# A hybrid encoder layer on one core: reordered gate and attention steps, two early weights in other tiles, normalisations at high priority

## The chip, the cores and the metric

The kernel runs on one core of one Trainium2 chip, in one launch. The metric is the device time of one execution in microseconds (us), median over the runs. The engines are TensorE (PE in the rows), VectorE (DVE), ScalarE (ACT) and GpSimd (POOL); SyncE (SP) issues most of the DMAs.

## The reference

One layer of an encoder over a sequence of 1024 tokens with 1024 features, all float32:

```python
u = rmsnorm(h, norm_mix_pre)
proj = u @ w_in                       # q, k, v, gate ga, low-rank za of the GLA heads; q, k, v of the window heads
o_a = gla_chunked(fwd) + flip(gla_chunked(bwd))          # 4 heads, chunks of 64, both directions
o_a = rms_per_head(o_a) * gla_norm * silu(ga)
o_s = banded_window_gqa(qs, ks, vs, sink, rel_table)     # 8 query heads, 2 kv heads, |i-j| <= 128
h = h + rmsnorm(concat([o_a, o_s]) @ w_out, norm_mix_post)
z = rmsnorm(h, norm_mlp_pre) @ w_up                      # 1024 x 4096
ff = square(relu(z)) @ w_down                            # 4096 x 1024
out = h + rmsnorm(ff, norm_mlp_post)
```

## The kernel before, in words

Every large matrix product is made of three: each float32 operand is split into a rounded high part (a cast) and the rest (a subtraction), and hi·hi, hi·lo and lo·hi are summed in PSUM. A weight that comes in therefore costs a DMA into a raw tile, a cast of 128x1024 on ACT (line 93) and a subtraction on DVE (line 196). PSUM is four tags of two banks each: "mm", "ga", "tr", "lg".

A scheduler sets the order of each engine's instructions when the program is built: of what could go next it takes what stands first in the program, and what is written under `tc.high_priority()` ahead of that. On the chip each engine runs its list in order. The program's order in the middle of the kernel is a string, `ORDER`, of tokens:

- `g<h><half>` is the gate projection of head h for one half of the tokens: 24 matmuls of 512 columns (line 222, `pin`), Silu on ACT (L648), a product on DVE (L649), and a store. Its weights are the tiles `wh` and `wl` (two buffers each), and the next head's weights are fetched when both halves of a head are done. `g0<half>` to `g3<half>` are eight such blocks.
- `S` is one step of the window attention, a unit of 128 queries and one kv head (16 units, software-pipelined): four logit products (`pl`, L545 and L546, tag "lg"), each reduced on DVE (L548) and put through the exponential on ACT (L551), a normalisation (L562), four groups of three transposes (`ppt`, L171, tag "tr"), each cast on ACT (L93) and subtracted on DVE (L571), and the product with v (`pvo`, L579 to L583, tag "lg"), copied out by ACT (L585). Silu and the exponential need different ACT tables, and a switch is an `ACT_TABLE_LOAD`.
- `W<k>`, `w<k>` load and split the k-th block of rows of w_out (512 KB; blocks 4 to 7 in two DMAs of 256 KB). Their raw tiles, of two buffers, are those of the gate weights.
- `M<n>` is w_out's product for tokens 128n to 128n+127, 48 matmuls of 512 columns (`pm`, L809 and L814), behind a load of the mixer's output (L800), a cast of it on ACT (L801) and a subtraction (L802). `N<n>` is the normalisation behind it (two squares on ACT at L825, a power on POOL at L180 and L181, DVE at L831 and L833, another square, DVE at L840), and `T<n>` transposes the result for the MLP (`pzt`, eight transposes, with copies on ACT at L856 and L859 and DVE work at L862 to L868).

After the string the MLP's first products stand in the program. `early(j)` brings columns of w_up into a raw tile and splits them into parts of `r1` and `r2`; `t_split` splits sums of the transposed tokens (L881, L882); `product(p, j)` is 12 matmuls of 512 columns (L995, into `pa`, `pb`, `pc`), written (p,j) below. The eighth normalisation takes two of the splits between its parts:

```python
early(0)
early(1)
t_setup()
wout_norm(7, pms[7], (lambda: t_split(0), lambda: t_split(1)))
```

In the profile the stretch of the gates is 285 to 347 us, that of M0 to M6 about 347 to 442 us, and the tail, from M7 to the first products of the MLP, 442 to 482 us. What follows to the end, some 600 us, is the MLP, whose program the change leaves as it is but for the place of one weight.

Of the kernel before, what the change touches and what calls it, by code (L numbers as in the profile page):

```python
# [20 lines left out]
S = 1024  # L21
# [50 lines left out]

ORDER = (
# [4 lines left out]
)  # L78


def hybrid_layer(tc, x, g_mix_pre, w_in, w_gu_f, b_g_f, w_gu_b, b_g_b, gla_norm, sink, rel_bias, w_out,
# [16 lines left out]
    with ExitStack() as ctx:  # L98
# [93 lines left out]
        def split(raw, hi, lo):  # L192
            k = spl_i[0]
            spl_i[0] += 1
            C(W_HI[k] if k < len(W_HI) else "a", hi, raw)
            E(W_LO[k] if k < len(W_LO) else "v").tensor_sub(lo, raw, hi)
# [231 lines left out]
        for tok in START.split():  # L428
            k, a = tok[0], tok[1:]
# [4 lines left out]
            elif k in "zvk":  # L434
                q0, n = int(a[0]), int(a[1])
# [14 lines left out]
        W2 = e2(8.25, 1056)  # L450
# [322 lines left out]
        wb = {}  # L773
# [40 lines left out]
                    nc.tensor.matmul(pm[c], lhsT=OTL[:, kt, :], rhs=woh[kt][:, sl], start=False, stop=kt == 7)  # L814
            return pm

        def wout_norm(n, pm, between=(None, None)):
            GB1, GB2 = wb["GB1"], wb["GB2"]

            TB, XB = wb["OT"] if n == 7 else (wb["TB"], wb["XB"])  # L820
            Q("xres").dma_start(XB, x[0, n * 128:(n + 1) * 128, :])
            s2 = tiny(2)
            for c in range(2):
                junk = wb["AR"](16, 512) if n > 4 else TB[:, c * 512:c * 512 + 512]
                nc.scalar.activation(junk, pm[c], AF.Square, scale=1.0 / 32, accum_out=s2[:, c:c + 1])  # L825
            r = rstd_of(s2[:, 0:1], 1, s2[:, 1:2])
            if between[0]:
                between[0]()
            for c in range(2):
                sl = slice(c * 512, c * 512 + 512)  # L830
                nc.vector.scalar_tensor_tensor(out=TB[:, sl], in0=pm[c], scalar=r, in1=GB1[:, sl],  # L831
                                               op0=ALU.mult, op1=ALU.mult)
            nc.vector.tensor_add(XB, XB, TB)  # L833
            Q("hds").dma_start(hd[n], XB)
            ss = tiny(1)
            nc.scalar.activation(TB, XB, AF.Square, scale=1.0 / 32, accum_out=ss)
            r = rstd_of(ss)
            if between[1]:
                between[1]()
            nc.vector.scalar_tensor_tensor(out=TB, in0=XB, scalar=r, in1=GB2, op0=ALU.mult, op1=ALU.mult)  # L840

        def wout_tr(n):
# [41 lines left out]
        pms = {}  # L884
        for tok in order:
            k, a = tok[0], tok[1:]
            if k == "K":
                proj_qk(int(a), "K", KD, 1.0)
            elif k == "Q":
                proj_qk(int(a), "Q", QD, 0.125)  # L890
            elif k == "H":
                gates(int(a))
            elif k in "VER":
                {"V": gla_v, "E": gla_e, "R": gla_r}[k](int(a))
            elif k in "CBF":
                {"C": gla_c, "B": gla_o, "F": gla_f}[k](int(a[0]), int(a[1]))
            elif k == "s":
                proj_qs(int(a))
            elif k == "S":
                swa_step()  # L900
            elif k == "L":
                load_bias()
            elif k in "Ww":
                fetch_wo(int(a))
            elif k == "g":
                ga_half(int(a[0]), int(a[1]))
            elif k == "M":
                pms[int(a)] = wout_mm(int(a))
            elif k == "N":
                wout_norm(int(a), pms[int(a)])  # L910
            elif k == "T":
                wout_tr(int(a))
            else:
                raise Stop(tok)
# [9 lines left out]
        def double(k):  # L924
            r, o = (r1, r2)[k % 4 // 2], 8 * (k % 2)
            return r(o, 1024), r(o + 4, 1024)
# [12 lines left out]
        def load_up(dst, f):  # L939
            nc.sync.dma_start(dst.rearrange("p (a b) -> p a b", a=8), w_up_r[:, :, f * 128:(f + 1) * 128])  # L940
# [2 lines left out]
            return t[:, i * 512:i * 512 + 512].rearrange("p (a b) -> p a b", a=4)  # L943

        def early(j):
            load_up(wb["RW"], j)
            split(double(j), wb["RW"])

        early(0)
        early(1)  # L950
        t_setup()
        wout_norm(7, pms[7], (lambda: t_split(0), lambda: t_split(1)))

        PA = [bank("mm", "pa0"), bank("mm", "pa1"), bank("ga", "pa2"), bank("ga", "pa3")]
        PB = [bank("lg", "pb0"), bank("lg", "pb1")]
# [20 lines left out]
        where = {}  # L976
# [9 lines left out]
            return PA[j % 4] if p in (1, 6, 7, 4) else PB[j % 2] if p == 2 else PC[j % 2]  # L986

        def product(p, j):
            (hi, lo), i = where[p, j] if p != 4 else (single(j), 0)
            hi, lo = k4(hi, i), k4(lo, i)  # L990
            bh, bl = U[tokens[p]]
            ps_ = bank_of(p, j)
            for n, (a, b) in enumerate(((hi, bh), (hi, bl), (lo, bh))):
                for kt in range(4):
                    nc.tensor.matmul(ps_, lhsT=a[:, kt, :], rhs=b[:, kt, :], start=p in (1, 2, 5) and n == 0 and kt == 0,  # L995
                                     stop=n == 2 and kt == 3, skip_group_check=True)
# [230 lines left out]
        for n, (i, u) in enumerate(steps):  # L1227
            p, _, _, banks = plan[i]
# [93 lines left out]
```

## Time and profile before

| what | value |
|---|---|
| median of 3 runs | 1080.88 us (1080.38 to 1081.57) |
| profiled execution, device time | 1081.89 us |
| its span in the trace | 1080.2 us |
| mean granted TensorE clock | 0.997 |
| PE busy | 1046.8 us (97%) |
| DVE busy | 723.5 us (67%) |
| ACT busy | 545.0 us (50%) |
| POOL busy | 154.7 us (14%) |
| chain that ended last | PE 82%, DVE 7%, ACT 3%, DMA 3% |

Busy shares are averages over the whole span. A matmul's busy time overlaps the next one's, so the distance from one start to the next tells what it takes on PE; where that is longer than the usual distance for its shape, PE lost the difference. The device time is 1.7 us longer than the span, for what lies around it.

### The profile page before, as it was taken

Reading aid. Unit: us, or ns where it says so; the run is one execution under the profiler, and the core shown is the slowest. Engines: PE = TensorE matmul, PEld = TensorE weight load, DVE = VectorE, ACT = ScalarE, POOL = GpSimd, SP = SyncE. Lnnn points to the kernel's source line nnn. Section 1 sums busy time; section 2 is a strip of 40 time slices with the busy share of each in tenths; the row PEclk is TensorE's granted clock in tenths of the full one; section 3 lists DMA queues with packets and bytes.
Section 4 is the critical chain, followed back from the end, with each engine's and each line's share of the span. In section 5 each row is a group of like instructions: output and inputs, shape, how many; then the busy total and the mean of one; then the engine's idle time right before and its main releaser. Section 6 shows DMA issues by size and latency. Waiting matters only on the chain.

```text
span 1080.2 us, 13661 instructions
## 1 busy us (share of the span) xinstructions
PE 1046.8 (97%) x4950; PEld 853.4 (79%) x4950; DVE 723.5 (67%) x1101; ACT 545.0 (50%) x952; POOL 154.7 (14%) x246
## 2 busy tenths in 40 slices
PE   6999999999998999989999999999999999999997
PEld 4787787887886887778888888888778888888885
DVE  8659457788778567799656656663479764547565
ACT  5565324633877456566555555554434334345342
POOL 4211012111211111102211212121100000002001
PEclk9999999999999999999999999999999999999999
DMA  7355443613667433547553635447983332345622
GB/s 229 114 158 164 133 124 83 147 40 82 178 182 182 120 121 103 160 121 237 195 171 118 193 117 172 151 138 241 381 320 99 97 98 98 117 137 185 204 98 98
DMA packets 138421, 164.82 MB, mean 153 GB/s; under 512 B 17089, under 2 KB 93889, under 8 KB 138354
## 3 DMA queue, kind: packets, MB, share of 16 engines
q1 hardware_dynamic: 109394, 110.46, 32.9%
q0 software_dynamic: 22560, 37.76, 11.9%
q10 hardware_dynamic: 6400, 15.73, 4.5%
q8 instruction: 39, 0.64, 0.3%
q14 instruction: 28, 0.23, 0.1%
HBM read 111.47 MB, written 52.45 MB: 152 GB/s over the span
## 4 chain that ended last, share of the span: by engine, by line
PE 82%; DVE 7%; ACT 3%; DMA 3%; issue 3%; POOL 1%; SPq 0%; ACTq 0%; DVEq 0%; POOLq 0%
PE pa L995 15%; PE pa L1219 15%; PE pin L222 11%; PE pc L995 8%; PE pb L1219 6%; PE pc L1219 6%; PE pm L809 3%; PE pb L995 3%; PE pm L814 2%; PE pkv L222 2%; PE ppt L171 2%; DMA wd<-in_w_down_dram 1%; PE pl L545 1%; PE pl L546 1%; PE pvo L579 1%
## 5 line engine op out<-in xcount | busy, mean ns | idle before, releaser
L1219 PE MATMUL pa<-r 128*128 128x512 f32 x768 | 175.1, 389 | 0.8 <-DVE r L1164 0.8
L1219 PEld LDWEIGHTS pa<-r 128*128 128x128 f32 x768 | 144.0, 188 | 31.4 <-DVE r L1164 1.6
L1161 ACT CAST r<-ra 128x1024 fp32r<-128x1024 f32 x56 | 58.9, 1052 | 166.0 <-PE pa L1219 94.2
L1163 DVE TENSOR_TENSOR r<-ra,r 128x1024 fp32r<-128x1024 f32 x56 | 68.4, 1222 | 106.7 <-ACT r L1161 106.7
L995 PE MATMUL pa<-th,r 128*128 128x512 f32 x384 | 102.3, 389 | 1.3 <-ACT sn L1010 1.3
L995 PEld LDWEIGHTS pa<-th,r 128*128 128x128 f32 x384 | 72.0, 188 | 16.6 <-ACT sn L1010 1.7
L222 PE MATMUL pin<-uth,wh 128*128 128x512 f32 x256 | 69.7, 398 | 0.0
L1219 PE MATMUL pb<-r 128*128 128x512 f32 x288 | 69.7, 390 | 0.0
L1219 PE MATMUL pc<-r 128*128 128x512 f32 x288 | 69.2, 389 | 0.0
L222 PE MATMUL pin<-utl,wh 128*128 128x512 f32 x256 | 68.2, 394 | 0.0
L222 PE MATMUL pin<-uth,wl 128*128 128x512 f32 x256 | 68.0, 394 | 0.0
L1164 DVE TENSOR_TENSOR r<-wd,r 128x1024 fp32r<-128x1024 f32 x52 | 63.3, 1217 | 4.4 <-ACT r L1162 4.4
L809 PE MATMUL pm<-wo,b 128*128 128x512 f32 x256 | 65.0, 396 | 0.0
L1219 PEld LDWEIGHTS pb<-r 128*128 128x128 f32 x288 | 53.9, 188 | 11.8 <-DVE r L1164 0.7
L1219 PEld LDWEIGHTS pc<-r 128*128 128x128 f32 x288 | 54.0, 188 | 11.2
L1069 DVE TENSOR_TENSOR r<-su,r 128x1024 fp32r<-128x1024 f32 x32 | 39.0, 1220 | 28.8 <-ACT r L1068 28.8
L180 POOL TENSOR_SCALAR cst<-cst 128x1 f32<-128x1 f32 x16 | 9.9, 618 | 337.5 <-ACT wd L1186 292.8
L1162 ACT CAST r<-wd 128x1024 fp32r<-128x1024 f32 x52 | 54.6, 1050 | 6.0 <-DMA wd<-in_w_down_dram 6.0
L1003 ACT ACTIVATE ar<-ar 128x512 f32<-128x512 f32 x42 | 26.5, 632 | 58.3 <-DVE ar L1014 58.3
L222 PEld LDWEIGHTS pin<-uth,wl 128*128 128x128 f32 x256 | 47.7, 188 | 9.0
L222 PEld LDWEIGHTS pin<-utl,wh 128*128 128x128 f32 x256 | 47.7, 188 | 8.9
L809 PEld LDWEIGHTS pm<-wo,b 128*128 128x128 f32 x256 | 47.1, 188 | 8.6
(291 smaller groups left out, 2121.5 us busy)
## 6 DMA issues: line engine op xcount, KB each, us to landing
ra<-hss SPq DMA_DIRECT2D x32, 512.0 KB, 3.7
wd<-in_w_down_dram SPq DMA_DIRECT2D x28, 512.0 KB, 9.1
hss<-ar POOLq DMA_DIRECT2D x54, 256.0 KB, 4.8
ra<-hsx SPq DMA_DIRECT2D x24, 512.0 KB, 3.6
hsx<-ar POOLq DMA_DIRECT2D x47, 256.0 KB, 2.8
ra<-in_w_up_dram SPq DMA_DIRECT2D x16, 512.0 KB, 4.1
rb<-in_w_up_dram SPq DMA_DIRECT2D x16, 512.0 KB, 5.7
raw<-in_w_in_dram SPq DMA_DIRECT2D x14, 512.0 KB, 4.5
```

Source lines behind the costliest of these rows:

```text
L171: nc.tensor.transpose(dst_bank[:, i * 128:(i + 1) * 128], s, ident)
L222: nc.tensor.matmul(p[:, cs], lhsT=a[:, kt, :], rhs=b[:, kt, cs], start=k == 0, stop=k == 23)
L809: nc.tensor.matmul(pm[c], lhsT=OTH[:, kt, :], rhs=w_[kt][:, sl], start=(w_ is woh and kt == 0), stop=False)
L814: nc.tensor.matmul(pm[c], lhsT=OTL[:, kt, :], rhs=woh[kt][:, sl], start=False, stop=kt == 7)
L995: nc.tensor.matmul(ps_, lhsT=a[:, kt, :], rhs=b[:, kt, :], start=p in (1, 2, 5) and n == 0 and kt == 0, stop=n == 2 and kt == 3, skip_grou ...
L1003: nc.scalar.activation(x_, x_ if src is None else src, AF.Relu)
L1069: late.append(lambda: nc.vector.tensor_sub(d[1], src, d[0]))
L1161: nc.scalar.copy(sd[0], ra[n % 2])
L1162: nc.scalar.copy(td[0], src)
L1163: nc.vector.tensor_sub(sd[1], ra[n % 2], sd[0])
L1164: nc.vector.tensor_sub(td[1], src, td[0])
L1219: nc.tensor.matmul(banks[t], lhsT=sd[a][:, c * 512 + t * 128:c * 512 + t * 128 + 128], rhs=td[b][:, c * 512:c * 512 + 512], start=p in (1, ...
```

## The change

Three edits. In `ORDER`, the steps between `g01` and `M0` are rearranged: the halves 0 of the gates (`g10`, `g30`, `g20`) come earlier, each with `W` tokens behind it, and of the six `S` there three remain; the three others now stand one behind `T1` and two behind `T2`. `early(3)` uses the tile `TB`, which the normalisations free, as its raw tile in place of `RW`, and `early(2)` is split in two halves, of which product (1,2)'s part goes to `single(0)`, a part of `r1` that nothing else holds so early. And `wout_norm` runs under `tc.high_priority()`, with the two splits behind the eighth and not between its parts.

```diff
-        "Q1 F11 E2 V2 C20 C21 R2 S S B20 B21 E3 V3 F21 F20 C30 C31 R3 S S g00 B30 B31 F31 g01 S F30 S W0 S "
-        "g11 g30 W1 g31 g10 W2 W3 g20 w4 w5 S S w6 g21 S w7 M0 N0 M1 T0 S N1 M2 T1 N2 M3 T2 N3 M4 T3 S S M5 "
-        "N4 T4 M6 N5 T5 N6 M7 T6 "
+        "Q1 F11 E2 V2 C20 C21 R2 S S B20 B21 E3 V3 F21 F20 C30 C31 R3 S S g00 B30 B31 F31 g01 F30 S W0 g10 W1 "
+        "g30 S W2 g11 W3 g20 w4 w5 g31 S w6 w7 g21 M0 N0 M1 T0 S N1 M2 T1 S N2 M3 T2 S S N3 M4 T3 S S M5 N4 T4 M6 "
+        "N5 T5 N6 M7 T6 "
...
-        def wout_norm(n, pm, between=(None, None)):
+        def wout_norm(n, pm):
...
-            if between[0]:
-                between[0]()
...
-            if between[1]:
-                between[1]()
...
-                wout_norm(int(a), pms[int(a)])
+                with tc.high_priority():
+                    wout_norm(int(a), pms[int(a)])
...
         def early(j):
-            load_up(wb["RW"], j)
-            split(double(j), wb["RW"])
+
+            raw = wb["TB" if j == 3 else "RW"]
+            load_up(raw, j)
+            if j == 2:
+                hi, lo = double(j)
+                split(single(0), raw[:, 0:512])
+                split((hi[:, 512:1024], lo[:, 512:1024]), raw[:, 512:1024])
+            else:
+                split(double(j), raw)
...
-        wout_norm(7, pms[7], (lambda: t_split(0), lambda: t_split(1)))
+        with tc.high_priority():
+            wout_norm(7, pms[7])
+        t_split(0)
+        t_split(1)
...
-            (hi, lo), i = where[p, j] if p != 4 else (single(j), 0)
+            (hi, lo), i = where[p, j] if p != 4 and (p, j) != (1, 2) else (single(j if p == 4 else 0), 0)
```

What this does to the engines' lists, at three places. (A number behind a name is the buffer's; the same tile may have another in the two kernels.)

**Place 1, ACT where head 2's gate weights are cast.** Of the kernel before, ACT's list: `pin_2685` is g31, `pin_2720` is g10, `wh_2715` are head 2's weights, `wo` is w_out.

```order
L93 CAST wo_2554<-raw_2748 128x1024
L551 ACTIVATE s2_85,cst_63<-s2_85,cst_63 128x384
L557 ACTIVATE cst_63<-cst_63 128x4
L585 COPY s3_525<-pvo_2604 64x512
L648 ACT_TABLE_LOAD
L648 ACTIVATE g3_517<-pin_2685 128x512
L93 CAST wh_2715<-raw_2713 128x1024
L93 CAST wo_2554<-raw_2752 128x1024
L648 ACTIVATE g3_517<-pin_2720 128x512
```

Of the kernel with the change, the same engine and place: `pin_2625` is g11, the last to read the buffer that head 2's weights `wh_2655` take, and `raw_2659` is the load of `W3`.

```order
L557 ACTIVATE cst_63<-cst_63 128x4
L93 CAST wo_2490<-raw_2659 128x1024
L585 COPY s3_525<-pvo_2602 64x512
L648 ACT_TABLE_LOAD
L648 ACTIVATE g3_517<-pin_2625 128x512
L93 CAST wh_2655<-raw_2653 128x1024
L93 CAST s1_89<-ppt_2735 128x3x128
L551 ACT_TABLE_LOAD
```

PE's list there, of the kernel before (g31's end, g10 and g20):

```order
L222 MATMUL pin_2685<-utl_78,wh_2413 128x512
L222 MATMUL pin_2720<-uth_75,wh_2092 128x512 x8
L222 MATMUL pin_2720<-uth_75,wl_2093 128x512 x8
L222 MATMUL pin_2720<-utl_76,wh_2092 128x512 x8
L222 MATMUL pin_2757<-uth_75,wh_2715 128x512 x8
```

And of the kernel with the change (g11's end to g20):

```order
L222 MATMUL pin_2625<-utl_78,wh_2092 128x512
L171 MATMUL ppt_2735<-cst_63,s2_85 128x128 x3
L545 MATMUL pl_2741<-s0_88 128x384
L546 MATMUL pl_2741<-s0_88,qz_526 128x384
L171 MATMUL ppt_2746<-cst_63,s2_85 128x128 x3
L545 MATMUL pl_2752<-s0_88 128x384
L546 MATMUL pl_2752<-s0_88,qz_526 128x384
L545 MATMUL pl_2763<-s0_88 128x384
L546 MATMUL pl_2763<-s0_88,qz_526 128x384
L222 MATMUL pin_2664<-uth_75,wh_2655 128x512 x8
```

Before, the cast of head 2's weights had g10's 24 matmuls beside it on PE; now it has two groups of transposes and three logit pairs.

**Place 2, PE ahead of M0.** Of the kernel before, the end of g21 (`pin_2931`) and the attention unit behind it:

```order
L222 MATMUL pin_2931<-utl_78,wh_2715 128x512 x2
L545 MATMUL pl_2880<-s0_88 128x384
L546 MATMUL pl_2880<-s0_88,qz_526 128x384
L545 MATMUL pl_2891<-s0_88 128x384
L546 MATMUL pl_2891<-s0_88,qz_526 128x384
L171 MATMUL ppt_2885<-cst_63,s2_85 128x128 x3
L171 MATMUL ppt_2896<-cst_63,s2_85 128x128 x3
L545 MATMUL pl_2902<-s0_88 128x384
L546 MATMUL pl_2902<-s0_88,qz_526 128x384
L579 MATMUL pvo_2907<-s1_89 128x512
```

Of the kernel with the change, g21 (`pin_2808`) to M0's first matmuls (`pm0_2853`):

```order
L222 MATMUL pin_2808<-utl_78,wh_2655 128x512 x2
L580 MATMUL pvo_2779<-s1_89 64x512
L579 MATMUL pvo_2779<-s1_89 128x512
L580 MATMUL pvo_2779<-s1_89 64x512
L582 MATMUL pvo_2779<-s1_89 64x512
L583 MATMUL pvo_2779<-s1_89 128x512
L222 MATMUL pin_2808<-utl_78,wh_2655 128x512 x4
L545 MATMUL pl_2993<-s0_88 128x384
L546 MATMUL pl_2993<-s0_88,qz_526 128x384
L545 MATMUL pl_3004<-s0_88 128x384
L546 MATMUL pl_3004<-s0_88,qz_526 128x384
L809 MATMUL pm0_2853<-wo_2490,b3_2840 128x512 x4
```

The unit's `pvo` now stands inside g21's matmuls; only two logit pairs of the next unit stand between g21 and M0.

**Place 3, PE in the tail.** Of the kernel before, T6 (`pzt_3806`, `pzt_3812`), four products, T7 (`pzt_3945`, `pzt_3951`), and the next products:

```order
L171 MATMUL pzt_3806<-cst_63,tb_3033 128x128 x4
L171 MATMUL pzt_3812<-cst_63,tb_3033 128x128 x4
L995 MATMUL pa0_3856<-b11_3028,r1_3823 128x512 x12
L995 MATMUL pb0_3860<-b21_3029,r1_3823 128x512 x12
L995 MATMUL pa1_3857<-b11_3028,r1_3823 128x512 x12
L995 MATMUL pb1_3861<-b21_3029,r1_3823 128x512 x12
L171 MATMUL pzt_3945<-cst_63,b2_3031 128x128 x4
L171 MATMUL pzt_3951<-cst_63,b2_3031 128x128 x4
L995 MATMUL pa2_3858<-b11_3028,r2_3824 128x512 x12
L995 MATMUL pb0_3860<-b21_3029,r2_3824 128x512 x12
L995 MATMUL pa3_3859<-b11_3028,r2_3824 128x512 x12
```

Of the kernel with the change, from T6 on (the ten matmuls that `pa0` and `pb0` lack here stand ahead of M7; line 995 is now line 1002):

```order
L171 MATMUL pzt_3806<-cst_63,tb_2841 128x128 x4
L171 MATMUL pzt_3812<-cst_63,tb_2841 128x128 x4
L1002 MATMUL pa0_3856<-b11_2836,r1_3823 128x512 x8
L1002 MATMUL pb0_3860<-b21_2837,r1_3823 128x512 x6
L1002 MATMUL pa1_3857<-b11_2836,r1_3823 128x512 x12
L1002 MATMUL pb1_3861<-b21_2837,r1_3823 128x512 x12
L171 MATMUL pzt_3947<-cst_63,b2_2839 128x128 x4
L171 MATMUL pzt_3953<-cst_63,b2_2839 128x128 x4
L1002 MATMUL pa2_3858<-b11_2836,r1_3823 128x512 x12
L1002 MATMUL pa3_3859<-b11_2836,r2_3824 128x512 x8
L1002 MATMUL pb0_3860<-b21_2837,r2_3824 128x512 x12
L1002 MATMUL pa3_3859<-b11_2836,r2_3824 128x512 x4
```

Product (1,2), `pa2`, now reads `r1` and not `r2`, and (1,3), `pa3`, comes ahead of (2,2), `pb0`.

## Rows read from the trace of the kernel before

**Rows 1.** Windows: PE, PEld, DVE, ACT, POOL busy (x), clock, DMA share, GB/s.

```profile
285.00:343.00 58.00, 54.16 (x271) 43.14 (x269) 46.10 (x108) 48.08 (x93) 10.09 (x15) 1.00 0.82 205
343.10:347.00 3.90, 3.90 (x15) 3.02 (x16) 2.48 (x8) 3.06 (x6) 0.00 (x0) 0.62 0.20 57
442.00:482.00 40.00, 35.88 (x166) 28.86 (x165) 34.25 (x41) 24.21 (x41) 4.79 (x8) 1.00 0.44 135
```

**Rows 2.** Timeline of PE, gates: start, duration, instruction, [idle before, releaser].

```profile
304.65 0.33 PE L545 MATMUL pl<-s 128*128 128x384 f32 x1
...
305.00 0.40 PE L580 MATMUL pvo<-s 128*64 128x512 f32 x1
...
335.51 0.82 PE L171 MATMUL ppt<-cst,s 128*128 128x128 f32 x6
336.08 0.71 PE L222 MATMUL pin<-utl,wh 128*128 128x512 f32 x2
...
339.09 0.34 PE L546 MATMUL pl<-s,qz 128*128 128x384 f32 x1
343.10 0.80 PE L579 MATMUL pvo<-s 128*128 128x512 f32 x1 [3.67 <-ACT s L93]
```

**Rows 3.** Timeline of ACT, gates.

```profile
328.60 1.05 ACT L93 CAST wo<-raw 128x1024 fp32r<-128x1024 f32 x1 [1.65 <-DMA raw<-in_w_out_dram]
...
337.79 1.28 ACT L648 ACT_TABLE_LOAD   x1
339.09 0.60 ACT L648 ACTIVATE g<-pin 128x512 f32<-128x512 f32 x1
339.70 1.28 ACT L551 ACT_TABLE_LOAD   x1
...
342.58 0.46 ACT L93 CAST s<-ppt 128x384 fp32r<-128x384 f32 x1
```

**Rows 4.** DMA issues of 285 to 345: count, KB each, median us to landing.

```profile
raw<-in_w_out_dram SPq DMA_DIRECT2D x8, 256.0 KB, 5.4
...
raw<-in_w_out_dram SPq DMA_DIRECT2D x3, 512.0 KB, 3.6
```

**Rows 5.** Timeline of PE, w_out's products with attention units between.

```profile
377.60 1.08 PE L809 MATMUL pm<-wo,b 128*128 128x512 f32 x4
378.82 0.55 PE L171 MATMUL ppt<-cst,s 128*128 128x128 f32 x3
...
417.20 0.86 PE L809 MATMUL pm<-wo,b 128*128 128x512 f32 x3
418.48 0.41 PE L171 MATMUL ppt<-cst,s 128*128 128x128 f32 x2 [0.43 <-DVE s L571]
```

**Rows 6.** Timeline of PE, tail.

```profile
449.59 3.79 PE L814 MATMUL pm<-wo,b 128*128 128x512 f32 x16
454.67 1.09 PE L171 MATMUL pzt<-cst,tb 128*128 128x128 f32 x8 [1.29 <-DVE tb L840]
...
461.08 2.88 PE L995 MATMUL pa<-b,r 128*128 128x512 f32 x12
463.80 2.88 PE L995 MATMUL pb<-b,r 128*128 128x512 f32 x12
467.33 1.09 PE L171 MATMUL pzt<-cst,b 128*128 128x128 f32 x8 [0.65 <-DVE b L840]
469.60 3.01 PE L995 MATMUL pa<-b,r 128*128 128x512 f32 x12 [1.18 <-ACT r L936]
472.45 2.88 PE L995 MATMUL pb<-b,r 128*128 128x512 f32 x12
476.34 3.06 PE L995 MATMUL pa<-b,r 128*128 128x512 f32 x12 [1.00 <-ACT r L936]
```

**Rows 7.** Timeline of DVE, tail.

```profile
467.19 1.22 DVE L882 TENSOR_TENSOR tl<-zf,th 128x1024 fp32r<-128x1024 f32 x1
468.32 1.22 DVE L882 TENSOR_TENSOR tl<-ar,th 128x1024 fp32r<-128x1024 f32 x1
```

## The prediction

> **What bounds the kernel now.** I read the busy shares first: PE is at work for 97% of the span, so an edit that leaves PE's work alone can only win back time that PE loses. The order of PE shows the same matmuls before and after (same shapes and counts), so the forecast is an account of PE's lost time in three stretches: gates, w_out's products, tail. Windows show how much is lost, and PE's timeline where: I took the distance from one start to the next and compared it with the usual distance of that shape.
>
> The usual distances: 12 matmuls of 512 columns take 463.80 − 461.08 = 2.72 us, so 0.227 each [rows 6]; a logit pair, L545 and L546, takes 305.00 − 304.65 = 0.35 [rows 2]; six transposes 336.08 − 335.51 = 0.57 [rows 2].
>
> *Gates.* In 285 to 343 us PE is idle for 58.00 − 54.16 = 3.84 [rows 1], and nearly all of it is one gap: the last logit matmul starts at 339.09, ends its slot at 339.27, and the next start is 343.10, so 3.83 [rows 2]. ACT tells why: a table load, g21's Silu, a table load back, then the exponentials and casts up to 342.58, for the last of which `pvo` waits [rows 3]. Nothing else was left for PE, since g21 was done. After it the granted clock is 0.62 for 3.90 us [rows 1], so between the two levels (1.2 and 2.4 GHz); against full speed that costs 3.90 × 0.38 = 1.48. And ahead of the gap the unit runs with no gate matmuls between: from 336.08 to 339.27, 3.19, PE does two matmuls (0.45), three logit pairs (1.05) and six transposes (0.57), 2.07 in all, so 1.1 is lost. Gates: 3.83 + 1.48 + 1.1 = **6.4**.
>
> *w_out's products.* Two places: four matmuls from 377.60 should end at 378.51, the next starts at 378.82: 0.31. Three from 417.20 end at 417.88, the next starts at 418.48: 0.60, released by DVE [rows 5]. Together **0.9**, with three attention units in the stretch.
>
> *Tail* [rows 6]. M7's last 16 matmuls end at 449.59 + 16 × 0.227 = 453.22, T6 starts at 454.67: 1.45 (its normalisation is late on DVE). T7: 463.80 + 2.72 = 466.52 to 467.33, 0.81. Product (1,2): the eight transposes take about 0.80, so 468.13 to 469.60, 1.47, waiting for ACT's cast of its weights. (1,3): 472.45 + 2.72 = 475.17 to 476.34, 1.17, the same for the next weights. Together **4.9**.
>
> **The change, part by part.**
>
> *Order of the gates.* The 3.83 gap and the bare unit go: the unit's `pvo` stands inside g21's matmuls (place 2). Two waits come in their place.
>
> First, g20. Head 2's weights take the buffer of head 1's, so they are cast only when g11 ends. Before, g10's 24 matmuls stood between (24 × 0.227 = 5.4 us of cover); now PE has six transposes and three logit pairs, 0.57 + 1.05 = 1.62 (place 1). On ACT a W3 cast, a copy, a table load, g11's Silu and then the cast of the weights stand in a row. If W3 has landed, ACT's chain behind g11's end is the rest of the copy (0.4, estimated as a Silu of the same width, 0.60, less the matmul behind it), 1.28, 0.60, and 1.05 less overlap [rows 3]: about 3.2, a wait of 3.2 − 1.62 = **1.55 at least**. W3's load is issued only when W2's raw tile is free, some 4 us ahead of g11's end by my reading of the order. With 3.6 to landing [rows 4] W3's cast of 1.05 falls about on g11's end and pushes the chain by 0.85: a wait of **2.4**, which I take, because 3.6 is the row of a 512 KB load of this matrix. With the 5.4 of the half-size loads [rows 4] it is 5.4 − 3.6 = 1.8 more: **4.1 at most**. That such loads can be late here is shown by a cast of `wo` that waited 1.65 for one [rows 3]. Behind the waiting casts stand a Silu and the next unit's exponentials, for which the next `pvo` waits; it has g20's 24 matmuls as cover.
>
> Second, M0. Behind g21 PE has two logit pairs, 0.70. M0 needs a cast of 1.05 (`b3`), which on ACT stands behind the casts of w6 and w7, the copy of `pvo`, a table load and g21's Silu. With all but Silu and cast done by g21's end: 0.60 + 1.05 + 0.15 for hand-overs − 0.70 = **1.1 at least**. With the copy and the table load falling behind g21's end, as `pvo` is written only four matmuls ahead of it: 0.6 + 1.28 − 4 × 0.227 = 1.0 more, and half a microsecond for the casts of w6, w7 ahead: **2.5**, which I take. With w7's load late by as much as the later W above (1.65): **4.2 at most**.
>
> After: 2.4 + 2.5 = 4.9, between 2.65 and 4.1 + 4.2 + 1.5 (the low clock once more) = 9.8. I take no low clock: behind the waits of 1.45 and 1.47 the tail's granted clock is 1.00 on the whole, behind the one of 3.83 it is 0.62 [rows 1], and 2.5 is nearer to the first. **Gain 6.4 − 4.9 = 1.5.**
>
> The order has two more table loads (15 for 13). In the trace a table load takes 1.28, and the next ACT instruction starts right behind it: 337.79 + 1.28 = 339.07, Silu at 339.09 [rows 3]. The two extra ones lie beside gate matmuls but for those counted above.
>
> The Trainium skill speaks against this part: its page "ScalarE: Activation LUTs", section "What ACT_TABLE_LOAD costs", puts a switch at some 1283 ns and a drain of about 1380 ns more, 2.66 us. By that rule the one table load on g20's way would be 1.38 dearer and, as an estimate by that page, the sum would end at 1079.0 rather than 1077.6. The trace shows the load's 1283 ns and no such drain.
>
> *Attention units in w_out's stretch.* Three units lose 0.9 there now, 0.3 each [rows 5]; six units would lose 1.8. M7 also starts about 0.2 late by the order, as its input's cast stands behind the normalisation's squares: 2.0. At least it stays at 0.9 (the M matmuls cover everything), at most each of four units waits at its four logit pairs as one does at 417.88, 4 × 4 × 0.60 = 9.6. I take 2.0, nearer the rows' mean of a unit than to its one worst wait. **Loss 1.1.**
>
> *Early weights and priority.* N6's squares now stand ahead of T5's copies on ACT, so T6's 1.45 goes. (1,2)'s weights go to a part of `r1` that is free long before, and (1,3)'s come by a tile of their own, which T6 frees some 9 us ahead: 1.47 and 1.17 go. What comes: ten product matmuls stand ahead of M7 (place 3), so T7 is reached 2.27 + 1.45 earlier after M7 than before, while N7's chain loses the splits that stood in it. These about cancel; T7's wait, or a late third load through `RW` whose cast stands in front of N7's second square on ACT, is between 0 and 2.4; I take 0.9, next to T7's 0.81 now. Behind T7, (2,2) needs `pb0`, which DVE reads behind four residuals of 1.13 (468.32 − 467.19 [rows 7]) and half of one, with two smaller sums ahead: 4.5 + 0.6 + 1.2 + 0.6 = 6.9 from N7's end, against PE's 0.80 + 2.72 + 8 × 0.227 = 5.3. With N7's end about a microsecond ahead of T7's transposes it waits 0.65. The next product behind it waits for `t_split(3)`, 0.45. Tail after 0.9 + 0.65 + 0.45 = 2.0, between 1.1 (no wait at T7) and 3.5. **Gain 4.9 − 2.0 = 2.9.** The split of `early(2)` makes two casts and two residuals of 512 columns out of one of 1024 each; ACT is idle for 15.8 of the tail's 40 us and DVE for 5.8 [rows 1], and only the residual counted above stands ahead of something PE waits for.
>
> **The sum.** 1.5 − 1.1 + 2.9 = 3.3 less than the profiled execution's 1081.89, so 1078.6. That execution stands 1.0 above the median of the runs; on the median's basis it is **1077.6** (0.3% below 1080.88).
>
> **The rivals.**
>
> *A, the waits are absorbed.* ACT is ahead of what I assume: gates lose 2.65, w_out's stretch 0.9, the tail 1.1. Gain 3.75 + 0 + 3.8 = 7.5, 1073.4. For it: ACT is busy for 48 of 58 us in the gates [rows 1], with fewer exponentials there after the change. Against it: the cast of head 2's weights can't start before g11's end.
>
> *B, the gates give nothing.* W3 and w7 are late as for the cast that waited [rows 3], and the clock falls again: the gates lose 9.8, 3.4 more than before. −3.4 − 1.1 + 2.9 = −1.6: 1082.5, no change that can be measured. For it: DMA is busy for 0.82 of the stretch [rows 1]. Against: fewer attention loads compete there now.
>
> *C, slower: w_out's stretch becomes DVE's and the banks' stretch.* Six units with N's high-priority work ahead of theirs on DVE: the logit banks come free late, as at 418.48 [rows 5]. Four units at 2.4 each lose about 10; 1.5 − 9.1 + 2.9 = −4.7, so 1085.7. Without gain is the change once that stretch loses more than 0.9 + 1.5 + 2.9 = 5.3, slower by 0.2% from 7.5 on. Against: one unit in three shows such a wait now, and once.
>
> That the change doesn't do what it says is excluded by the order: the moves are there.
>
> **Chances and range.** Two medians of this kernel can be told apart from about 0.2% on, 2.2 us: faster is below 1078.7, slower above 1083.0. My forecast has 0.55, its own range being 1075.5 to 1079.7; A 0.18, B 0.17, C 0.10. Faster: two thirds of the forecast's (0.37) and A: 0.55. The same: the rest of the forecast's and nearly all of B: 0.33. Slower: C and a little of B: 0.12. The range reaches from A to B, 1073.4 to 1082.5, and leaves out C and the outer sides of A and B.
>
> **What would show it.** In the profile after: no gap of over 3 us behind the last gate; a gap of about 2.4 ahead of g20's first matmul, released by ACT's cast of `wh` or DVE's residual, and one of about 2.5 ahead of M0, released by the cast of `b`; waits of 0.3 to 0.6 at the logits of six units in w_out's stretch; T6 without a wait, (1,2) and (1,3) without one for their weights; small waits at T7, (2,2) and `t_split(3)`. It is wrong if the granted clock falls behind one of the two gaps, if w_out's stretch loses over 5, or if a transfer through `RW` or `TB` lands behind N7.

## The result, and the profile after

The kernel with the change takes 1089.49 us (median of 6 runs, 1086.65 to 1091.27) against 1081.16 before (6 runs). The ratio is 1.0074, with a 95% interval of 1.0062 to 1.0087: 8 us slower, where 3.3 us of gain were forecast. The profiled execution has a span of 1087.5 us, 7.3 more than before.

The windows of the kernel after, with the columns of [rows 1]:

```profile
285.00:343.00 58.00, 50.66 (x241) 40.48 (x240) 38.73 (x80) 44.44 (x73) 6.75 (x10) 0.96 0.75 193
...
350.00:442.00 92.00, 88.49 (x443) 70.43 (x442) 63.80 (x138) 55.27 (x137) 15.77 (x28) 1.00 0.37 106
...
316.00:318.00 2.00, 1.68 (x7) 1.42 (x8) 2.00 (x5) 1.97 (x4) 0.00 (x0) 1.00 0.91 268
338.00:340.00 2.00, 0.00 (x0) 0.00 (x0) 0.00 (x0) 0.00 (x0) 0.00 (x0) 0.62 0.62 185
340.00:342.00 2.00, 0.71 (x2) 0.62 (x3) 0.73 (x1) 1.04 (x1) 0.00 (x0) 0.50 0.00 0
```

In 285 to 343 us PE is idle for 7.34 us where before it was for 3.84 [rows 1], in w_out's stretch for 3.51 of 92, and the granted clock, 1.00 behind g20's wait (the row of 316 us), falls to 0.50 (the lower of its two levels) by 340 us. With every start on PE compared with the usual distance of its shape, as in the prediction, PE loses: in the gates (285 to 348 us) 11.0 us where it was 7.4, in w_out's stretch (348 to 445) 6.2 where it was 2.3, and in the tail (445 to 490) 4.4 where it was 5.2. These windows are a little wider than the prediction's list of single waits, whose sums for before were 6.4, 0.9 and 4.9. The rest of the 7.3 lies in stretches that the change doesn't touch.

PE's timeline after, at the places that answer to [rows 2, 5, 6]:

```profile
312.27 0.49 PE L171 MATMUL ppt<-cst,s 128*128 128x128 f32 x3
314.72 0.44 PE L545 MATMUL pl<-s 128*128 128x384 f32 x1 [1.96 <-DVE s L586]
...
316.32 0.96 PE L222 MATMUL pin<-uth,wh 128*128 128x512 f32 x3 [0.45 <-ACT wh L93]
...
336.14 0.33 PE L546 MATMUL pl<-s,qz 128*128 128x384 f32 x1
341.29 4.89 PE L809 MATMUL pm<-wo,b 128*128 128x512 f32 x12 [4.81 <-ACT b L801]
...
365.88 3.66 PE L809 MATMUL pm<-wo,b 128*128 128x512 f32 x15
370.23 0.52 PE L171 MATMUL ppt<-cst,s 128*128 128x128 f32 x3 [0.69 <-DVE b L858]
...
375.20 0.55 PE L171 MATMUL ppt<-cst,s 128*128 128x128 f32 x3 [0.18 <-DVE s L571]
...
465.18 1.03 PE L171 MATMUL pzt<-cst,tb 128*128 128x128 f32 x8
...
476.17 1.32 PE L171 MATMUL pzt<-cst,b 128*128 128x128 f32 x8 [1.32 <-DVE b L836]
...
483.11 3.01 PE L1002 MATMUL pb<-b,r 128*128 128x512 f32 x12 [0.72 <-DVE ar L1021]
```

Three things are to be seen. Ahead of g20 (316.32) PE loses 2.12 at the logits and 0.61 at the cast of `wh`, 2.7 in all, about as forecast (2.4). Ahead of M0 (341.29) it loses 4.97, twice the forecast. And in w_out's stretch each T that has a unit behind it ends with a wait of 0.8 at the unit's first transposes, for the bank that DVE's residual of T (L858) frees, and one of 0.35 to 0.43 later; there are four such pairs, together 4.8 us. In the tail T6 has no wait and (1,2), (1,3) none of over 0.21, as forecast; T7 waits 1.49 and (2,2) 0.88.

What M0 waited for stands in ACT's timeline and SP's. ACT's, with a row of w_out's stretch that is used below:

```profile
336.40 0.60 ACT L648 ACTIVATE g<-pin 128x512 f32<-128x512 f32 x1
340.20 1.04 ACT L801 CAST b<-b 128x1024 fp32r<-128x1024 f32 x1 [3.20 <-DMA otd<-g]
...
366.89 0.59 ACT L855 CAST b<-pzt 128x512 fp32r<-128x512 f32 x1
```

SP's DMA issues:

```profile
331.13 1.20 SPq L800 DMA_DIRECT2D b<-otd  x2
337.75 0.36 SPq L650 DMA_DIRECT2D otd<-g  x1
```

The cast of M0's input (340.20) is released by the DMA that stores g21's product, issued at 337.75, and not by the load of its input, issued at 331.13. The cast's target lies in the 8 KB tile G3 in which the gates keep their staging, and a tile can be taken over only when its last user is done, which is the store's landing; the cast starts 2.45 us behind the store's issue. In the kernel before the same rule held, but there an attention unit stood between g21 and M0, and the time of that unit, with its own gap of 3.83 [rows 2], covered the store. SP's issue of it there, and ACT's cast, which starts before the unit is through on PE:

```profile
341.93 0.36 SPq L650 DMA_DIRECT2D otd<-g  x1
```

```profile
344.58 1.06 ACT L801 CAST b<-b 128x1024 fp32r<-128x1024 f32 x1
```

DVE's timeline after, at the wait at 370.23:

```profile
368.08 1.41 DVE L829 SCALAR_TENSOR_TENSOR tb<-pm,cst,b 128x512 f32<-128x512 f32 x2 [1.50 <-POOL cst L181]
369.41 0.68 DVE L858 TENSOR_TENSOR b<-pzt,b 128x512 fp32r<-128x512 f32 x1
```

DVE stands still for 1.50 us, waiting for POOL's power, with the normalisation's two products at the head of its list; T's residual, whose input ACT has cast by 367.48 (366.89 + 0.59), stands behind them and starts at 369.41. It frees the bank at 370.1, and PE goes on at 370.23. POOL's power itself is this, of its timeline:

```profile
367.48 0.56 POOL L181 TENSOR_TENSOR cst<-cst 128x1 f32<-128x1 f32 x1
```

### The profile page after: what moved, and what is told of

It reads as the page before. It is cut to its first block, busy times and chain, and to the rows that moved or that the text cites. A ratio compares the mean times of both kernels' runs of the same rounds, so it can differ in the third digit from the quotient of the medians.

```text
span 1087.5 us, 13649 instructions
## 1 busy us (share of the span) xinstructions
PE 1050.6 (97%) x4950; PEld 855.3 (79%) x4950; DVE 722.6 (66%) x1102; ACT 549.4 (51%) x955; POOL 160.0 (15%) x246
## 4 chain that ended last, share of the span: by engine, by line
PE 81%; DVE 8%; issue 3%; DMA 3%; ACT 3%; POOL 2%; SPq 0%; ACTq 0%; DVEq 0%; POOLq 0%
PE pa L1226 16%; PE pa L1002 15%; PE pin L222 12%; PE pc L1002 8%; PE pb L1226 6%; PE pc L1226 6%; PE pb L1002 3%; PE pm L809 2%; PE pm L814 2%; PE pkv L222 2%; PE ppt L171 1%; DMA raw<-in_w_in_dram 1%; POOL cst L181 1%; PE pl L545 1%; DVE tb L836 1%
## 5 line engine op out<-in xcount | busy, mean ns | idle before, releaser
L809 PE MATMUL pm<-wo,b 128*128 128x512 f32 x256 | 67.9, 407 | 4.8 <-ACT b L801 4.8
L180 POOL TENSOR_SCALAR cst<-cst 128x1 f32<-128x1 f32 x16 | 13.0, 815 | 337.3 <-ACT wd L1193 287.3
```

Of the source, the lines that this page charges most:

```text
L180: nc.gpsimd.tensor_scalar(r, ss, more, EPS, op0=ALU.add, op1=ALU.add)
L809: nc.tensor.matmul(pm[c], lhsT=OTH[:, kt, :], rhs=w_[kt][:, sl], start=(w_ is woh and kt == 0), stop=False)
```

## Experiments

The theory after the result had two parts: the order costs the gates (M0 behind g21's store), and the priority costs w_out's stretch. The first four runs take the three edits apart.

**The order alone.** The edit to the kernel before:

```diff
-        ... g00 B30 B31 F31 g01 S F30 S W0 S g11 g30 W1 g31 g10 W2 W3 g20 w4 w5 S S w6 g21 S w7 M0 N0 M1 T0 S N1 M2 T1 N2 M3 T2 N3 ...
+        ... g00 B30 B31 F31 g01 F30 S W0 g10 W1 g30 S W2 g11 W3 g20 w4 w5 g31 S w6 w7 g21 M0 N0 M1 T0 S N1 M2 T1 S N2 M3 T2 S S N3 ...
```

> The kernel before with the new order string alone (no priority, early weights as before). Theory (the order costs the gates 3.7 us, since M0 waits 5 us behind g21 for the store of g21's product, and the priority of the normalisations costs w_out's stretch most of its 4 us): slower than before by about 4.5 us, 1085.5, with the gap of 4 to 5 ahead of M0 in the trace and waits of at most 0.4 at the units' transposes. Rival (six units in w_out's stretch instead of three are the cost, whatever the priority): slower by about 8, 1089, with waits of 0.8 at the transposes.

Measured: ratio 1.0043 (1.0027 to 1.0059), 4.7 us slower, as the theory had it. PE's timeline of it ahead of M0:

```profile
334.33 0.33 PE L546 MATMUL pl<-s,qz 128*128 128x384 f32 x1
340.57 1.65 PE L809 MATMUL pm<-wo,b 128*128 128x512 f32 x3 [5.91 <-ACT b L801]
```

The gap ahead of M0 is there, larger than in the full change. w_out's stretch loses 2.05 us, less than the 2.3 before, with six units in it instead of three: at ordinary priority six units cost no more than three.

**The priority alone.** The kernel before with `with tc.high_priority():` around `wout_norm` and the two splits behind the eighth.

> The kernel before with the normalisations at high priority alone (and the two splits behind the eighth). Theory: the three units in w_out's stretch wait 0.8 to 1.2 each for banks that DVE frees late (about 2.5 us lost), the tail wins T6's 1.45 us: near no change, 1081 to 1083. Rival: no cost in w_out's stretch, the tail's gain stands alone: faster by 1.5 to 2, 1079.

Measured: ratio 1.0001 (0.9988 to 1.0014), no change. PE's timeline shows both halves of the theory's sum, the waits at the transposes and, not shown here, T6 without its 1.45:

```profile
378.26 0.52 PE L171 MATMUL ppt<-cst,s 128*128 128x128 f32 x3 [0.65 <-DVE b L858]
...
383.23 0.55 PE L171 MATMUL ppt<-cst,s 128*128 128x128 f32 x3 [0.32 <-DVE s L571]
```

w_out's stretch loses 3.7 (2.3 before), the tail 4.2 (5.2 before). In the old order only two T have a unit behind them, and the waits there come to 0.81 and 0.48 for the first and 0.87 and 0.35 for the second, 2.5 us for two where the change has 4.8 for four. So the price of the priority for each such T is about the same with either order, 1.2 to 1.3 us; with the old order the gain in the tail and the 0.9 us of waits that stood there before nearly pay for it.

**The early weights alone.** `early`, and the place of (1,2)'s weights, as in the change; the rest as before.

> The kernel before with the two early weights in their other homes alone. Both theories: products (1,2) and (1,3) no longer wait for their weights (1.47 and 1.17 us), T6 and T7 wait as before: faster by 1.5 to 2.6, about 1079. If the waits only move to the next products, as the prediction's 0.65 and 0.45 behind T7 would have it, faster by about 1.

Measured: 1078.71 us, ratio 0.9971 (0.9961 to 0.9981), 3.1 us faster, a little over the upper end. The tail of it on PE:

```profile
467.81 1.09 PE L171 MATMUL pzt<-cst,b 128*128 128x128 f32 x8 [0.42 <-DVE b L840]
468.65 2.78 PE L1002 MATMUL pa<-b,r 128*128 128x512 f32 x11
471.37 3.00 PE L1002 MATMUL pb<-b,r 128*128 128x512 f32 x12
474.21 2.88 PE L1002 MATMUL pa<-b,r 128*128 128x512 f32 x12
```

Behind T7 the products follow one another without a wait, where before there were 1.47 and 1.17 [rows 6]. This part of the change is a gain.

**The change without priority on N0 to N6.**

```diff
-                with tc.high_priority():
-                    wout_norm(int(a), pms[int(a)])
+                wout_norm(int(a), pms[int(a)])
```

> The kernel with the change, but without high priority on the first seven normalisations (the eighth keeps it). Theory: the waits of 0.8 at the units' first transposes go, about 3.4 us: 1086 against 1089.5. Rival (density of the units): the waits stay, 1089 to 1090.

Measured: 1083.13 us, ratio 1.0015 (1.0005 to 1.0025). Against the change's 1.0074 that is 0.6%, 6.4 us, more than the theory's 3.4. w_out's stretch loses 1.95 instead of 6.2, and the tail 1.8 instead of 4.4. The sum of order and early weights alone, 4.7 − 3.1 = 1.6, is what this run shows (1.6). So priority costs nothing on balance with the old order and over 6 us with the new one.

The next five runs go after the gap ahead of M0.

**Two staging tiles for one.** The 8 KB tile G3 becomes two of 4 KB, so that M0's cast takes over the one that g31 used last:

```diff
-        VF = [g3(0, 512), g3(2, 512)]
+        VF = [g3(0, 512), g3b(0, 512)]
...
-        gst = [g3(4, 512), g3(6, 512)]
+        gst = [g3(2, 512), g3b(2, 512)]
...
-            b3 = slot("G3", 8, F32R, "b3")
+            b3, b3b = slot("G3", 4, F32R, "b3"), slot("G3b", 4, F32R, "b3b")
```

> The kernel with the change, but with the 8 KB tile that holds the gates' staging, and after them the cast input of M0, made of two tiles of 4 KB, one for even and one for odd gate blocks, so that M0's cast waits for the store of g31's product and no longer for g21's. Theory (the 5 us ahead of M0 are the store of g21's product, which must land before the cast may write there): the cast of M0's input starts right behind g21's Silu, the gap falls from 5.0 to about 1.7, the low clock behind it goes (about 2): 1084 to 1085 against 1089.5. Rival (M0 waits for the load of its input, issued 10 us earlier): the gap stays at 4 or more, 1088 to 1090.

Measured: 1084.91 us, ratio 1.0040 (1.0026 to 1.0055). The gap falls from 4.97 to 2.52, not to 1.7, and the low clock behind it is shorter but not gone. SP's timeline of it, and then ACT's:

```profile
331.98 1.29 SPq L802 DMA_DIRECT2D b<-otd  x2
338.60 0.36 SPq L652 DMA_DIRECT2D otd<-g3b  x1
```

```profile
337.25 0.60 ACT L650 ACTIVATE g3b<-pin 128x512 f32<-128x512 f32 x1
338.59 1.04 ACT L803 CAST b<-b 128x1024 fp32r<-128x1024 f32 x1 [0.74 <-DVE g3b L651]
```

The cast starts at 338.59, before the store of g21 is even issued. That the store held M0 is shown. It isn't the whole gap: the cast still comes 0.74 behind the Silu. The engine named is a product that nothing of this tile needs; M0's load, issued at 331.98, takes 6.51 to landing by the trace (its issue row is two loads merged), so it lands at 338.49, 0.10 ahead of the cast. The load is next in line; the next run's trace names it.

**Both: two staging tiles, no priority on N0 to N6.**

> The split staging tiles and no priority on the first seven normalisations, else the kernel with the change. If the two costs are independent: 1083.1 (the run without priority) less what the split wins, 4.5 to 6: 1077 to 1078.5, 0.3% faster than before. If the gap ahead of M0 has another cause: 1083.

Measured: 1077.69 us, ratio 0.9964 (0.9950 to 0.9979): 0.4% faster than before, as expected of two independent costs. Its 12 runs go from 1074.18 to 1081.19, and the profiled one, of 1081.19, is the slowest of them. In ACT's timeline the cast of M0's input now waits for its load:

```profile
338.15 1.04 ACT L803 CAST b<-b 128x1024 fp32r<-128x1024 f32 x1 [1.77 <-DMA b<-otd]
```

**A unit between g21 and M0 as cover** (no priority on N0 to N6):

```diff
- ... w4 w5 g31 S w6 w7 g21 M0 N0 ...
+ ... w4 w5 g31 w6 w7 g21 S M0 N0 ...
```

> Without priority on the first seven normalisations and with the attention step that stands ahead of w6 in the new order moved behind g21, so that a unit stands between g21 and M0 as in the kernel before. Theory: the store of g21 lands while the unit runs, but the unit itself waits for its exponentials behind two table loads, as before: the gap of 6 becomes one of 3.5 to 4, 1081 to 1082 against 1083.1. Rival (any cover heals the gap): 1077 to 1079.

Measured: 1081.06 us, ratio 1.0003 (0.9991 to 1.0014), the theory's 1081 to 1082. PE's timeline:

```profile
335.51 0.34 PE L546 MATMUL pl<-s,qz 128*128 128x384 f32 x1
340.45 0.80 PE L579 MATMUL pvo<-s 128*128 128x512 f32 x1 [4.60 <-ACT s L93]
```

The gap is the unit's own again, as in [rows 2]: 4.77 by the distance of the starts, where 3.5 to 4 was expected and the run without priority has 6.0. ACT's timeline tells what the unit waited for, and it isn't two table loads:

```profile
336.59 1.05 ACT L93 CAST wo<-raw 128x1024 fp32r<-128x1024 f32 x1 [1.11 <-DMA raw<-in_w_out_dram]
...
338.03 1.28 ACT L551 ACT_TABLE_LOAD   x1
```

One cast of w_out stood in front, late by 1.11 for its own load, and one table load behind it. So the time came out as expected, and the sum behind it did not. Cover that itself waits for ACT is little cover.

**g31 as cover of the weights' cast** (two staging tiles, no priority on N0 to N6):

```diff
- ... g11 W3 g20 w4 w5 g31 S w6 w7 g21 M0 N0 ...
+ ... g11 W3 g31 w4 w5 g20 S w6 w7 g21 M0 N0 ...
```

> As the split staging without priority, and with g31 and g20 changed places in the order, so that g31's 24 matmuls cover the cast of head 2's weights. Theory: the wait of 2.6 and 0.6 ahead of g20 goes and no other takes its place: 3 us below the run with split staging and no priority, about 1074.5. Rival (the wait goes on behind g20, since the attention unit's bank is the cause of 2 of it): less than 1 us below.

Measured: 1076.62 us (6 runs, 1076.17 to 1078.34), ratio 0.9961 (0.9948 to 0.9974). Against the run with the same staging and the order as changed, 1077.69, this is no clear gain, and not the 3 us of the theory (that run's profiled execution was the slowest of its 12, so the two traces don't compare in size). The wait at g20 is gone, but a wait of 1.34 at the transposes behind it and a longer gap ahead of M0 took over part of it:

```profile
333.64 0.34 PE L548 MATMUL pl<-s,qz 128*128 128x384 f32 x1
337.54 2.90 PE L811 MATMUL pm<-wo,b 128*128 128x512 f32 x8 [3.57 <-ACT b L803]
```

Its ratio is the lowest measured here, 0.39% faster than before, but those of the kernel with the order as changed (0.9964) and of the next run (0.9962) lie within its interval.

**M0's load alone in the queue** (the kernel of the run above, with one column copied from M0's input tile to M1's, so that M1's load waits for M0's):

```diff
+            if n == 1:
+                nc.vector.tensor_copy(wb["OT"][1][:, 0:1], wb["OT"][0][:, 0:1])
             Q("otf").dma_start(otf, otd[n // 4][n % 4].rearrange("k p c -> p k c"))
```

> The version with split staging, without priority and with g31 as cover, and M1's input load held until M0's has landed (one column copied from the one tile to the other orders them). Theory (the gap of 3.7 ahead of M0 that is left there is M0's load, which shares the queue with M1's of the same size): the load lands in 4.5 rather than 7 us, the cast stands right behind w7's, the gap falls to 2.9 and the clock falls less: about 1 below 1076.6. Rival (the load is not what is waited for): 1076.6.

Measured: 1077.62 us, ratio 0.9962 (0.9949 to 0.9975): no gain. The DMA view of the stretch and ACT's timeline:

```profile
b<-otd SPq DMA_DIRECT2D x1, 512.0 KB, 6.3
```

```profile
335.69 1.04 ACT L93 CAST wo<-raw 128x1024 fp32r<-128x1024 f32 x1
336.79 1.04 ACT L805 CAST b<-b 128x1024 fp32r<-128x1024 f32 x1
```

The gap ahead of M0 is 2.94, near the theory's 2.9, but not for its reason. Alone in the queue the load still takes 6.3 to landing (7.1 with M1's behind it in the run above), and not 4.5. Issued at 330.45, it lands at 336.72, just when w7's cast ends (336.73), so the trace can't tell which of the two the cast of M0's input waited for. Waits of 1.03 and 1.14 at attention steps beside g21 stand in this run's trace, and the time is the same.

The last four runs ask how the priority costs what it does.

**Priority on N0 to N4 and N7, not on N5 and N6.**

> The kernel with the change, with high priority on N0 to N4 and N7 but not on N5 and N6. Theory (two separate costs: 4.2 us where N0 to N4 hold DVE ahead of the residuals of T0 to T3, and 2.6 us in the tail, where priority puts ten product matmuls ahead of M7 instead of ahead of T6): w_out's stretch stays at 6, the tail falls from 4.4 to about 1.8: 1086.5 to 1087. Rival (the tail's cost comes from the late w_out stretch): tail stays, 1089.

Measured: ratio 1.0064 (1.0052 to 1.0077), 1089.3: no different from the change within the noise. w_out's stretch loses 5.9, the tail 5.8. The theory's second half is wrong twice: the tail's loss does not come from N5 and N6, and it is there with a single product matmul ahead of M7 in place of ten. PE's timeline of that one (M7's first matmul follows at 452.42):

```profile
450.83 0.39 PE L1002 MATMUL pb<-b,r 128*128 128x512 f32 x1
```

**Priority on N5, N6 and N7 alone.**

```diff
-                with tc.high_priority():
+                with (tc.high_priority() if int(a) >= 5 else ExitStack()):
```

> The kernel with the change, with high priority on N5, N6 and N7 alone. Theory: w_out's stretch falls from 6.2 to about 2, the tail stays at 4.4: about 1085. Rival: the waits at the transposes stay (the six units are their cause), 1089.

Measured: 1082.47, ratio 1.0016 (1.0003 to 1.0029), as without any priority on N0 to N6. w_out's stretch loses 2.15, the tail 2.4. So the whole 6 us hang on N0 to N4, the tail's part too. By which way the tail loses is not shown: of the runs with the new order and priority on N0 to N4 the change has ten product matmuls ahead of M7's end, but the run above has one and loses more there. DVE's timeline of this run, at the place of the rows of after:

```profile
366.25 0.69 DVE L858 TENSOR_TENSOR b<-pzt,b 128x512 fp32r<-128x512 f32 x1 [0.26 <-ACT zf L857]
...
369.82 0.75 DVE L829 SCALAR_TENSOR_TENSOR tb<-pm,cst,b 128x512 f32<-128x512 f32 x1 [0.37 <-POOL cst L181]
```

The residuals (the second starts at 367.23) run before POOL is done, at 369.79, the products follow, and PE's transposes at 367.00 and 368.07 have no wait. ACT's order differs too: here T's copies come ahead of N1's two squares, in the change behind them.

**T0 to T4 at high priority too.**

```diff
-                wout_tr(int(a))
+                with (tc.high_priority() if int(a) < 5 else ExitStack()):
+                    wout_tr(int(a))
```

> The kernel with the change, and T0 to T4 at high priority too, so that on DVE the two residuals of T stand ahead of the next normalisation's two products instead of behind and between them. Theory (DVE stands still for POOL's power at the head of its list while T's residual, whose input is there, stands behind it, and so the two transpose banks come free 0.85 late): the waits of 0.8 at the units' first transposes go, w_out's stretch loses 2 to 3 instead of 6.2, 1085.5 to 1087. Rival (DVE has too much work in that stretch in any order): no better than 1089.

Measured: ratio 1.0115 (1.0101 to 1.0129), 1094.4, a miss on the far side of both. PE's timeline:

```profile
363.59 1.09 PE L171 MATMUL pzt<-cst,tb 128*128 128x128 f32 x8 [1.36 <-DVE tb L836]
```

The edit moved T's transposes on PE as well, into the middle of the next product, where they wait for their own normalisation. It changed two things and tells nothing of one.

**Only T's copies and residuals at high priority** (T0 to T3; the transposes not), which moves the residuals ahead of the two products on DVE, and on ACT the copies in between the normalisation's two squares:

> The kernel with the change, and of T0 to T3 only the copies out of the two banks and their residuals at high priority, not the transposes: on DVE the two residuals stand ahead of the normalisation's two products, and PE's transposes stay where they are. Theory (DVE waits 1.5 us for POOL at the head of its list while the residual behind it is ready, and the units' transposes wait 0.85 for its bank): the four waits of 0.8 go, w_out's stretch loses 2.5 to 3.5 instead of 6.2, 1085.5 to 1087; if the tail's extra 2 us are carried on from there, 1084. Rival (DVE is too busy in any order): no better than 1089.

Measured: ratio 1.0092 (1.0075 to 1.0109), 1092.3, the rival's side. DVE's timeline, the next wait on PE, and POOL's power:

```profile
368.03 1.29 DVE L859 TENSOR_TENSOR b<-pzt,b 128x512 fp32r<-128x512 f32 x2 [1.33 <-ACT zf L858]
370.16 1.41 DVE L829 SCALAR_TENSOR_TENSOR tb<-pm,cst,b 128x512 f32<-128x512 f32 x2 [0.84 <-POOL cst L181]
371.48 0.55 DVE L571 TENSOR_TENSOR s<-ppt,s 128x384 fp32r<-128x384 f32 x1
```

```profile
372.08 0.55 PE L171 MATMUL ppt<-cst,s 128*128 128x128 f32 x3 [0.56 <-DVE s L571]
```

```profile
369.56 0.56 POOL L181 TENSOR_TENSOR cst<-cst 128x1 f32<-128x1 f32 x1
```

The waits at the first transposes are gone, as the theory had it, and reappear at the next ones: now it is the unit's own residual (L571) that stands behind the two products, and DVE still idles ahead of them, 0.84 us for POOL. That agrees with the products' early place in DVE's list being the cost, whichever residual stands behind them. It doesn't show it, since the edit moved a second thing: with T's copies between the squares POOL's power starts at 369.56 where it started at 367.48 in the change, and the products 2.1 us later, and so all that stands behind them.

## Why the prediction was wrong

*The sum.* It was 1.5 − 1.1 + 2.9 = +3.3. In the same stretches the traces show about −3.6 (gates), −3.9 (w_out's stretch) and +0.8 (tail). The result lies outside the range and beyond rival C's 1085.7. Of the signs that were named for being wrong, the clock fell behind one of the two gaps, and w_out's stretch loses 6.2 by the wider windows, 4.8 in the single waits.

*The steps that failed are the second wait of the gates, and the loss in w_out's stretch.*

1. *M0.* The prediction had 2.5, "which I take", and 4.2 at most. The wait is 4.97, 6.1 with the order alone. The chain was read from ACT's list (copy, table load, Silu, cast) and is right as far as it goes: Silu starts at 336.40. Left out was what the cast writes: a tile that the gates' staging holds until g21's product has been stored. DVE's product, the issue at 337.75 and the 2.45 us from there to the cast come in on top. The run with two staging tiles takes 2.45 of the gap away and 3.7 us of the time, since the low clock behind the gap is shorter too (0.86 in 342 to 344 us, where the change has 0.50). The 2.52 that is left there equals the 2.5 forecast by chance: 0.74 of it is the wait for the load of M0's input, which the prediction's sum doesn't have. Nothing in [rows 2, 3] shows the rule, since there the cast followed a cast of w_out and PE was at the unit; it stood only in the part of the code that hands the tile G3 on.

2. *The clock.* "I take no low clock": behind the first part of M0's gap the granted clock is 0.62, then 0.50. That it would not fall was an argument from the tail's waits of 1.45 and 1.47. The gap was longer than the 2.5 that was weighed, but the argument from size doesn't hold either: ahead of g20 it fell behind waits of 1.27 and 0.61 in one run and not behind 2.12 and 0.61 in the change (see the last section).

3. *w_out's stretch.* "Three units lose 0.9 there now, 0.3 each [rows 5]; six units would lose 1.8." The order alone has six units there and loses 2.05, in fact nothing more than before. So the step that failed is the price by the number of units. The cost is the priority of N0 to N4, which the prediction weighed in the tail alone: without it the stretch loses 1.95 to 2.15, with it 5.9 to 6.2. Rival C had the place, DVE and the banks, and the cause, "N's high-priority work ahead of theirs on DVE", with a price of 10 and a chance of 0.10; the measured price is 4.

4. *The tail.* T6, (1,2) and (1,3) went as forecast, and the early weights alone give 3.1 us. T7 waits 1.49 where I took 0.9, (2,2) 0.88 where I took 0.65. The part of it that is lost again, about 2 us, hangs on N0 to N4's priority, as the runs with priority on either group show. By which way is open: it does not need the ten product matmuls ahead of M7, as the run with one of them loses 5.8.

*What was right.* The wait ahead of g20 (2.4 forecast, 2.7 measured), with its mechanism: W3's load lands at 311.75, about when g11 ends, and the cast, copy, table load, Silu and cast of `wh` follow one another on ACT. Most of the wait shows at a logit, whose bank the same late copy holds; the cast of `wh` ends it. No drain behind a table load: behind 12 of the 13 loads in the kernel before the next instruction starts within 0.02 us of the load's end, as in [rows 3] (behind the other within 0.54), so the page "ScalarE: Activation LUTs" of the Trainium skill, section "What ACT_TABLE_LOAD costs", with its 1380 ns more, played no part.

*What stays open.* Which of N0 to N4's instructions makes the cost. The runs show that the priority of these five makes it, and that DVE idles for POOL with the two products at the head of its list while a ready residual stands behind them. Whether it is these products, or the two squares that stand ahead of T's copies on ACT, no run tells apart: neither was tried at ordinary priority by itself.

## What to carry to other kernels

Before a step is moved forward, look up which tile its first write takes over and who lets go of it last: that can be the landing of a store that no list of the waiting engine shows, and work that stood between the two by accident was its cover. High priority for a chain that passes through another engine puts its waiting instruction at the head of an in-order list; measure it together with the order it is used with, since here it cost nothing on balance with one order and 0.6% with another. Edits that come together are worth timing apart: one of the three was a gain of 0.3%.

## What the runs showed of the hardware that I had not expected

Waits of much the same size on PE can bring the lower clock or not. Ten of the profiled kernels keep the wait ahead of g20. In three of them, the change among them (waits of 2.12 and 0.61, a granted clock of 1.00 in the row of 316 us above), the clock stays up; in seven it falls. Windows of the run with two staging tiles (waits of 2.18 and 0.61), and then of the last run (1.27 and 0.61, the shortest of the ten):

```profile
316.00:318.00 2.00, 2.00 (x5) 1.63 (x6) 1.75 (x4) 1.97 (x3) 0.00 (x0) 0.50 1.03 262
```

```profile
316.00:318.00 2.00, 2.00 (x6) 1.59 (x5) 1.13 (x3) 1.99 (x5) 0.00 (x0) 0.50 1.05 252
```

So the length of the longest wait doesn't decide it; what does, the runs don't show, with one trace of each kernel. In the run with both remedies the clock falls behind M0's gap of 2.97 as well, and costs more than in the kernel after, because PE is back at work while it lasts:

```profile
340.00:342.00 2.00, 2.00 (x7) 1.52 (x6) 0.00 (x0) 0.00 (x0) 0.00 (x0) 0.50 0.13 39
```

In the kernel after PE is busy for 0.71 of the same 2 us. Over the 12 runs of the kernel with both remedies the mean granted clock goes with the time: 0.998 and 0.999 in the three fastest (1074.18 to 1075.15 us), 0.994 to 0.996 in the three slowest (1080.50 to 1081.19). So this kernel has a spread of 7 us of its own, as has the one with priority on N5, N6 and N7 alone (1080.67 to 1087.87), and one run of such a kernel tells little.
